# Two hybrid layers on one core: TensorE's order planned in the source by lanes, dilated heads ahead of the latent ones, full-row dilated scores, latent exponentials kept in PSUM

## The chip, the cores and the metric

The kernel runs on one core of one Trainium2 chip. The metric is the device time of one execution in microseconds (us); lower is better. The engines are called as the profile calls them: PE is TensorE (PEld its weight loads), DVE is VectorE, ACT is ScalarE, POOL is GpSimd, SP is SyncE, which issues the DMAs.

## What is computed

Two layers run one after the other over 1024 tokens of width 1024, all in float32. The first adds a pooling mixer and a sliding-window attention; the second adds a latent attention (8 heads, every key) and a dilated attention (24 heads in three groups with dilations 1, 4 and 16, merged by their log-sums). Cut to what matters here:

```python
def hybrid_layer(x, positions, ...):                      # the second layer
    h = rmsnorm_2(x, attn_norm_g)
    proj = h @ w_in
    (c_q, c_kv, k_rope, z_mla, q_dil, k_dil, v_dil, z_dil, g_mla, g_dil) = jnp.split(proj, ...)
    a_out = mla_attention(c_q, c_kv, k_rope, positions, ...)
    y_mla = (a_out * jax.nn.silu(z_mla)) @ w_o_mla
    d_out = dilated_mixture(q_dil, k_dil, v_dil, positions)
    y_dil = (d_out * jax.nn.silu(z_dil)) @ w_o_dil
    merged = sigmoid(g_mla + ...) * y_mla + sigmoid(g_dil + ...) * y_dil
    return x + merged @ w_out

def one_block(q_blk):                                     # latent attention, 128 queries
    s = jnp.einsum('bqhd,bkhd->bhqk', q_blk, k).astype(jnp.float32)
    p = jax.nn.softmax(s, axis=-1).astype(v.dtype)
    return jnp.einsum('bhqk,bkhd->bqhd', p, v)
```

The latent part and the dilated part both need only `h`; the outputs of both meet in `merged`.

## The kernel before

Each float32 operand of a product is split in a high part (a cast to the type `fp32r`) and a low part (the difference), and a product is the sum of high x high, high x low and low x high: three matmuls (`mm3`, lines 136 to 142). ACT makes the high part, DVE the low one (`sub_lo`, lines 115 and 116). A projection of 128 output columns over one half of the tokens is `proj_half` (line 147): 8 x 3 matmuls of 512 columns into one bank of PSUM; its weights come by `load_w` (line 130).

The stages, with the time in the profiled execution at which they stand: norm and transposes of the input (to 25 us), sliding-window attention and pooling (to 292), output projection and second norm (to 402), the small latent projections (to 541), the latent heads (to 986), the dilated heads (to 1600), the two gated output projections (to 1701) and the last projection with the final norm.

*Latent heads* (line 866 on). For each of 8 heads and each half of the queries, 8 key blocks: three score matmuls of 512 columns (891 to 893), exp from PSUM to an SBUF tile `E` (898), a cast to `ph` (901) and a subtraction to `pl` (902, helper line 116), and two block products later in the source the products with the values `vm` (885, 886). POOL adds the `E` tiles for the softmax denominator (907, 925), which `key_sums` (837) finishes with two matmuls of a column of ones. The next head's row maxima come from `row_max` (819), one 512-column matmul and one DVE reduction each; `max_rows` (826) transposes them, negates them and writes them by DMA into row 96 of q, so that the first scores of a head wait for that DMA. `fill()` (line 668) puts other projections (gates, z, v of the dilated heads) between.

*Dilated heads* (line 1093 on). Twelve units, each two heads of one dilation. A unit's q, k and v are projected, q and k turned by `roped` (line 953: a swap by DMA, a product on DVE, one on POOL, a sum on DVE). The q tile of a head holds the high part in the head's 64 rows and the low part in the other 64. k's high part is copied to both halves (`khd`), its low part `kl` is not. So a pair of score matmuls is one of 128 rows and one of 64:

```python
nc.tensor.matmul(o, U.qs[i][:, q], U.kh[i][:, k], start=True, stop=False)
nc.tensor.matmul(o, U.qs[i][r, q], U.kl[r, k], start=False, stop=True)
```

`Head.scores` and `Head.values` (lines 214 and 245) run the two attentions with narrow windows: a masked copy with its maximum on DVE, exp on ACT, transposes of P on PE (291), cast and subtraction (293, 294), products (267). `merge` (1040) joins the three groups of a head through DRAM into `d_d`, which the last stages read.

The order of PE's instructions is not the source's alone. The program is recorded under a scheduler that orders each engine's instructions by its own cost model; the source gives the order in which work is offered (the lists `MLA_FILL`, `MAXES`, `fillers`), and the pools of PSUM banks (`share_banks`, line 90) set how far work can run ahead.

Of the kernel before, what the change touches and what calls it, by code (L numbers as in the profile page):

```python
# [20 lines left out]
C_ID = 0  # L21
C_D1 = 128
C_W = 384
C_M2 = 768
C_IC = 896
C_FREQ = 960
# [41 lines left out]
def hybrid_kernel(  # L68
# [17 lines left out]
    sm = pool("sm", 4)  # L86
    banks = ctx.enter_context(ExitStack())
    pp = psS = psO = psT = None

    def share_banks(p, s, o, t=2):  # L90

        nonlocal pp, psS, psO, psT
        banks.close()
        pp = banks.enter_context(tc.tile_pool(name="pp", bufs=p, space=PSUM))
        psS = banks.enter_context(tc.tile_pool(name="psS", bufs=s, space=PSUM))
        psO = banks.enter_context(tc.tile_pool(name="psO", bufs=o, space=PSUM))
        psT = banks.enter_context(tc.tile_pool(name="psT", bufs=t, space=PSUM))
# [4 lines left out]
    xp = first.enter_context(tc.tile_pool(name="xp", bufs=1))  # L102
    x0 = [xp.tile([128, D], F32, name=f"x{t}") for t in range(8)]
    cc = cst.tile([128, C_N], F32, name="cc")
# [12 lines left out]

    background = []
# [50 lines left out]
    def norm_T(xt, gain, H, t):  # L169

        ss = sm.tile([128, 1], F32, tag="ss", name="ss")
        xn = P_p.tile([128, 1024], F32, tag="P", name="xn")
        nc.scalar.activation(out=xn, in_=xt, func=AF.Square, accum_out=ss)
        rs = rstd_of(ss, D)
        nc.vector.scalar_tensor_tensor(out=xn, in0=xt, scalar=rs, in1=gain, op0=ALU.mult, op1=ALU.mult)
        tok = slice(128 * t, 128 * t + 128)
        for a in range(2):
            ps = psT.tile([128, 4, 128], F32, tag="t", name="pst")
            for j in range(4):
                k = 4 * a + j  # L180
                nc.tensor.transpose(ps[:, j, :], xn[:, 128 * k:128 * k + 128], ident)
            hi = H[0][:, 4 * a:4 * a + 4, tok]
            nc.scalar.copy(hi, ps)
            sub_lo(nc.vector, H[1][:, 4 * a:4 * a + 4, tok], ps, hi)

# [6 lines left out]
    def V_natural(vt, v):  # L192

        for a in range(2):
            ps = psT.tile([128, 4, 2, 64], F32, tag="t", name="pst")
            for j in range(4):
                t = 4 * a + j
                nc.tensor.transpose(flat(ps[:, j]), vt[:, 128 * t:128 * t + 128], ident)
            hi = v[:, 4 * a:4 * a + 4, :, 0]
            nc.scalar.copy(hi, ps)  # L200
            sub_lo(nc.vector, v[:, 4 * a:4 * a + 4, :, 1], ps, hi)


    class Head:
# [6 lines left out]
        def __init__(self, scores_mm, v, tiles, keys, scale, mask, m, den, init=None, fill=()):  # L211
            self.__dict__.update(locals())

        def scores(self):
            self.nm = sm.tile([128, 8], F32, tag="nm", name="nm")
            self.P = []
            for half in range(2):
                P = P_p.tile([128, 4, 256], F32, tag="P", name="P")
                self.P.append(P)
                for (i, a, n) in self.fill:  # L220
                    if i // 4 == half:
                        nc.gpsimd.memset(P[:, i % 4, a:a + n], 0.0)
                for j in range(2):
                    ps = psS.tile([128, 2, 256], F32, tag="s", name="pss")
                    for u in range(2):
                        i = 4 * half + 2 * j + u
                        k0, kw, p0 = self.tiles[i]
                        self.scores_mm(ps[:, u, p0:p0 + kw], slice(128 * i, 128 * i + 128), slice(k0, k0 + kw))
                    for u in range(2):
                        i = 4 * half + 2 * j + u  # L230
                        k0, kw, p0 = self.tiles[i]
                        nc.vector.tensor_tensor_reduce(  # L232
                            out=P[:, 2 * j + u, p0:p0 + kw], in0=ps[:, u, p0:p0 + kw], in1=self.mask(i),
                            scale=1.0, scalar=-3e38 if self.init is None else self.init,
                            op0=ALU.add, op1=ALU.max, accum_out=self.m[:, i:i + 1])
                h4 = slice(4 * half, 4 * half + 4)
                nc.vector.tensor_scalar(out=self.nm[:, h4], in0=self.m[:, h4], scalar1=-self.scale, scalar2=None, op0=ALU.mult)  # L237
                for j in range(4):
                    i = 4 * half + j
                    k0, kw, p0 = self.tiles[i]  # L240
                    a = P[:, j, p0:p0 + kw]
                    nc.scalar.activation(out=a, in_=a, func=AF.Exp, bias=self.nm[:, i:i + 1], scale=self.scale,  # L242
                                         accum_out=self.den[:, i:i + 1])

        def values(self, dest):

            o = [None, None]
            last = {}
            for c, qs in enumerate(self.keys):
                for (i, _) in qs:  # L250
                    last[i // 4] = (c, i)
            opened = set()

            def accumulate(c, h, l, cols):
                runs = []
                for n, (i, _) in enumerate(self.keys[c]):
# [44 lines left out]
            for item in late:  # L301
                accumulate(*item)
# [975 lines left out]
```

## Time and profile before

| what | value |
|---|---|
| median of 3 runs | 1797.91 us (1795.03 to 1797.92) |
| the profiled execution | 1797.49 us |
| its span, first to last instruction | 1795.6 us |
| PE busy | 1712.9 us, 95%, 7900 records |
| PEld busy | 1380.6 us, 77% |
| DVE busy | 1107.9 us, 62% |
| ACT busy | 798.7 us, 44% |
| POOL busy | 430.0 us, 24% |
| DMA | 206.85 MB, mean 115 GB/s |

Busy time is the union of an engine's records. Records of PE overlap, because matmuls are pipelined: the length of one is longer than the step from its start to the next one's start. A time of the profiled execution is read against its own 1797.49 us.

### The profile page before, as it was taken

Reading aid. Unit: us, or ns where it says so; the run is one execution under the profiler, and the core shown is the slowest. Engines: PE = TensorE matmul, PEld = TensorE weight load, DVE = VectorE, ACT = ScalarE, POOL = GpSimd, SP = SyncE. Lnnn points to the kernel's source line nnn. Section 1 sums busy time; section 2 is a strip of 40 time slices with the busy share of each in tenths; the row PEclk is TensorE's granted clock in tenths of the full one; section 3 lists DMA queues with packets and bytes.
Section 4 is the critical chain, followed back from the end, with each engine's and each line's share of the span. In section 5 each row is a group of like instructions: output and inputs, shape, how many; then the busy total and the mean of one; then the engine's idle time right before and its main releaser. Section 6 shows DMA issues by size and latency. Waiting matters only on the chain. (4 is left out here: it accounts for less than half of the span.)

```text
span 1795.6 us, 22168 instructions
## 1 busy us (share of the span) xinstructions
PE 1712.9 (95%) x7900; PEld 1380.6 (77%) x7900; DVE 1107.9 (62%) x1840; ACT 798.7 (44%) x1622; POOL 430.0 (24%) x280
## 2 busy tenths in 40 slices
PE   7999998999999998998989999999999989999998
PEld 6788886888787885776867778777778767877786
DVE  5677764562645677767786576775775567345532
ACT  4455433342332454555555465555555445432121
POOL 1000010011332345546554220230230122032200
PEclk8999998999999998999999999999999989999999
DMA  5311126443344221423132634464463235378642
GB/s 180 80 36 49 49 93 196 136 124 74 88 156 141 68 75 28 113 77 113 50 92 75 166 95 108 119 176 112 114 165 89 76 98 141 126 242 279 188 138 85
DMA packets 189081, 206.85 MB, mean 115 GB/s; under 512 B 29107, under 2 KB 152179, under 8 KB 188844
## 3 DMA queue, kind: packets, MB, share of 16 engines
q1 hardware_dynamic: 188972, 205.45, 39.6%
q8 instruction: 62, 1.02, 0.2%
q14 instruction: 47, 0.39, 0.1%
HBM read 126.86 MB, written 52.27 MB: 100 GB/s over the span
## 5 line engine op out<-in xcount | busy, mean ns | idle before, releaser
L140 PE MATMUL pp<-Hh,whi 128*128 128x512 f32 x1248 | 498.8, 400 | 8.9 <-ACT rt L956 3.0
L142 PE MATMUL pp<-Hh,wlo 128*128 128x512 f32 x1248 | 495.9, 397 | 0.0
L141 PE MATMUL pp<-Hl,whi 128*128 128x512 f32 x1248 | 494.0, 396 | 0.0
L140 PEld LDWEIGHTS pp<-Hh,whi 128*128 128x128 f32 x1248 | 236.5, 190 | 61.3 <-ACT rt L956 4.3
L142 PEld LDWEIGHTS pp<-Hh,wlo 128*128 128x128 f32 x1248 | 236.3, 189 | 51.3 <-issue 0.5
L141 PEld LDWEIGHTS pp<-Hl,whi 128*128 128x128 f32 x1248 | 236.6, 190 | 47.6 <-DVE Hl L116 0.2
L126 ACT CAST whi<-wraw 128x1024 fp32r<-128x1024 f32 (+3 forms) x110 | 109.8, 999 | 221.5 <-PE pp L141 123.6
L116 DVE TENSOR_TENSOR wlo<-wraw,whi 128x1024 fp32r<-128x1024 f32 (+3 forms) x110 | 144.3, 1312 | 94.8 <-ACT whi L126 88.5
L907 POOL TENSOR_TENSOR E<-E 128x1024 f32<-128x1024 f32 x48 | 123.5, 2572 | 208.3 <-ACT E L898 103.2
L116 DVE TENSOR_TENSOR pl<-E,ph 128x512 fp32r<-128x512 f32 x128 | 150.9, 1206 | 31.6 <-ACT ph L901 16.7
L242 ACT ACTIVATE P<-P,nm 128x256 f32<-128x256 f32 (+2 forms) x256 | 118.7, 466 | 96.2 <-DVE nm L237 96.0
L960 POOL TENSOR_TENSOR rsw<-rsw,sinT 128x1024 f32<-128x1024 f32 x24 | 74.7, 3114 | 227.1 <-DMA rsw<-rt 183.0
L824 DVE TENSOR_REDUCE mx<-pst 128x1 f32<-128x512 f32 x128 | 85.5, 683 | 60.7 <-PE pst L823 60.2
L898 ACT ACTIVATE E<-pss 128x512 f32<-128x512 f32 x128 | 74.0, 598 | 71.2 <-PE pss L893 49.6
L116 DVE TENSOR_TENSOR pl<-pst,ph 128x512 fp32r<-128x512 f32 (+2 forms) x120 | 75.5, 639 | 36.1 <-ACT ph L293 35.6
L166 POOL TENSOR_TENSOR rs<-ms,mhalf 128x1 f32<-128x1 f32 (+1 forms) x40 | 23.1, 578 | 278.0 <-DVE ms L164 278.0
L901 ACT CAST ph<-E 128x512 fp32r<-128x512 f32 x128 | 76.6, 622 | 29.3 <-PE pso L885 20.0
L293 ACT CAST ph<-pst 128x512 fp32r<-128x512 f32 (+2 forms) x120 | 64.1, 549 | 54.4 <-PE pst L291 51.3
L232 DVE CUSTOM_DVE_ANT_0 P<-pss,cc 128x256 f32<-128x256 f32 (+2 forms) x192 | 62.6, 369 | 28.1 <-PE pss L1023 22.8
L267 PE MATMUL pso<-ph,v 128*128 128x256 f32 (+1 forms) x280 | 75.3, 287 | 2.5 <-ACT ph L293 2.3
L267 PE MATMUL pso<-pl,v 128*128 128x256 f32 (+1 forms) x280 | 69.4, 285 | 6.2 <-DVE pl L116 6.2
L1022 PE MATMUL pss<-khd,qs 128*128 128x256 f32 (+2 forms) x192 | 64.8, 337 | 6.3 <-DVE qs L116 6.0
(264 smaller groups left out, 3187.1 us busy)
## 6 DMA issues: line engine op xcount, KB each, us to landing
wraw<-in_w_in_dram SPq DMA_DIRECT2D x78, 512.0 KB
rsw<-rt SPq DMA_DIRECT2D x96, 128.0 KB
khd<-kh SPq DMA_DIRECT2D x48, 256.0 KB
wraw<-in_w_out_dram SPq DMA_DIRECT2D x16, 512.0 KB
g_d<-g SPq DMA_DIRECT2D x16, 512.0 KB
og_d<-og SPq DMA_DIRECT2D x12, 512.0 KB
ol<-og_d SPq DMA_DIRECT2D x12, 512.0 KB
bc<-b_d SPq DMA_DIRECT2D x24, 256.0 KB
```

The lines of the kernel that those rows point to most:

```text
L116: eng.tensor_tensor(out=lo, in0=src, in1=hi.bitcast(F32), op=ALU.subtract)
L126: nc.scalar.copy(wh, raw)
L140: nc.tensor.matmul(ps, lh, rh, start=(i == 0), stop=False)
L141: nc.tensor.matmul(ps, lh, rl, start=False, stop=False)
L142: nc.tensor.matmul(ps, ll, rh, start=False, stop=(i == n - 1))
L242: nc.scalar.activation(out=a, in_=a, func=AF.Exp, bias=self.nm[:, i:i + 1], scale=self.scale, accum_out=self.den[:, i:i + 1])
L267: nc.tensor.matmul(o[b][:, q0:q0 + 128 * w], self.v(c), part[:, cols + 128 * n:cols + 128 * (n + w)], start=b not in opened, stop=(part is ...
L824: nc.vector.tensor_reduce(out=mx[:, n, i:i + 1], in_=ps, axis=mybir.AxisListType.X, op=ALU.max)
L898: nc.scalar.activation(out=e, in_=ps, func=AF.Exp, scale=MSC)
L901: nc.scalar.copy(ph, e)
L907: nc.gpsimd.tensor_tensor(out=Es[0], in0=Es[0], in1=E, op=ALU.add)
L960: nc.gpsimd.tensor_tensor(out=sw, in0=sw, in1=sinT, op=ALU.mult)
```

## The change

The arithmetic is the same but for the order of some sums. Four things are different.

1. PE's order is taken from the source (`manual_schedule` for that engine). The source plans it: the stages are generators, "lanes", that yield what they wait for; a `Flow` keeps a clock of constants (.23 us per 512 columns, so much per ACT, DVE and POOL operation) and steps the lane of the lowest number whose needs are met, else the projections in `stream`, else it moves its clock. In the latent stage `pace` limits how many projections may go.
2. The dilated heads stand right behind the second norm, the latent projections and heads behind them. The v projections no longer pass through DRAM.
3. k's low part is copied to both halves as well, and the second score matmul takes all 128 rows.
4. The latent exp is written over its scores in PSUM; cast and subtraction read it there. The product of the high part runs on a bank of its own, that of the low part on another with only the high part of v and a column of ones, whose row is a part of the denominator; POOL adds the high parts alone.

```diff
+    ctx.enter_context(tc.manual_schedule(engines={mybir.EngineType.PE}))
...
+    class Flow:
+        HOP, SLACK = 0.15, 0.7
...
+        def mm(self, n, cols=512):
+            self.now += n * max(0.11, 0.23 * cols / 512)
...
+        def run(self, *until):
+
+            while any(l[2] is not None for l in until):
+                best = None
+                for lane in self.lanes:
+                    ts = [e.t for e in lane[2]]
+                    if None in ts:
+                        continue
+                    at = max(ts, default=0.0)
+                    at += self.SLACK if at > 0.0 else 0.0
+                    if at <= self.now:
+                        best = (self.now, lane)
+                        break
+                    if best is None or at < best[0]:
+                        best = (at, lane)
...
+                at, lane = best
+                if at > self.now:
+                    self.idle.append((self.now, at))
+                    self.now = at
+                self.step(lane)
...
-                nc.tensor.matmul(o, U.qs[i][:, q], U.kh[i][:, k], start=True, stop=False)
-                nc.tensor.matmul(o, U.qs[i][r, q], U.kl[r, k], start=False, stop=True)
+                nc.tensor.matmul(o, self.qs[i][:, q], self.kh[i][:, k], start=True, stop=False)
+                nc.tensor.matmul(o, self.qs[i][:, q], self.kl[i][:, k], start=False, stop=True)
...
+                            for (part, dup) in ((hi, self.kh[i]), (lo, self.kl[i])):
+                                for z in range(2):
+                                    nc.sync.dma_start(dup[64 * z:64 * z + 64].bitcast(F32), part[64 * i:64 * i + 64].bitcast(F32))
...
+    lanes = [F.add(score_lane(heads2), 8), F.add(turn_lane(heads2), 6), F.add(value_lane(heads2), 5)]
...
+    share_banks(4, 2, 0)
+    set_rings(4, 1, 0)
...
-                nc.scalar.activation(out=e, in_=ps, func=AF.Exp, scale=MSC)
-                nc.scalar.copy(ph, e)
-                sub_lo(nc.vector, pl, e, ph)
-                if kb % 2 and kb > 1:
-                    nc.gpsimd.tensor_tensor(out=Es[0], in0=Es[0], in1=E, op=ALU.add)
+                    pace[0] += 14 * MLA_TILES / 128
+                    nc.scalar.activation(out=ps, in_=ps, func=AF.Exp, scale=MSC)
+                    nc.scalar.copy(ph, ps)
+                    sub_lo(nc.vector, pl, ps, ph)
+                    elif kb > 1:
+                        nc.gpsimd.tensor_tensor(out=acc, in0=acc, in1=ph.bitcast(F32), op=ALU.add)
...
-                nc.tensor.matmul(o, v, ph, start=(kb == 0), stop=False)
-                nc.tensor.matmul(o, v, pl, start=False, stop=(kb == 7))
+                    nc.tensor.matmul(o, vm[:, kb, h, 0:128], ph, start=(kb == 0), stop=(kb == 7))
+                    nc.tensor.matmul(o2[0:65], vm[:, kb, h, 64:129], pl, start=(kb == 0), stop=(kb == 7))
...
+    pace[0] = 14 * MLA_FIRST
+    load_qk(0)
+    lanes = [F.add(product_lane(), 5), F.add(exp_lane(), 8), F.add(max_lane(), 7)]
```

Three places of PE's queue show what moved. A row is a source line, the operation, result and operands by the program's names, and the result's size. The first is in the dilated stage, at scores of a unit with 256-column tiles (`khd` and `kl` or `kld` are k's high and low part, `pp` a projection). Before:

```order
L291 MATMUL pst<-idt,P 128x128
L1022 MATMUL pss<-khd,qs 128x256
L1023 MATMUL pss<-kl,qs 128x256
L1022 MATMUL pss<-khd,qs 128x256
L1023 MATMUL pss<-kl,qs 128x256
L1022 MATMUL pss<-khd,qs 128x256
L1023 MATMUL pss<-kl,qs 128x256
L141 MATMUL pp<-Hl,whi 128x512
```

Now:

```order
L463 MATMUL pst<-idt,P 128x128 x8
L1133 MATMUL pss<-khd,qs 128x256
L1134 MATMUL pss<-kld,qs 128x256
L1133 MATMUL pss<-khd,qs 128x256
L1134 MATMUL pss<-kld,qs 128x256
L1133 MATMUL pss<-khd,qs 128x256
L1134 MATMUL pss<-kld,qs 128x256
L1133 MATMUL pss<-khd,qs 128x256
L1134 MATMUL pss<-kld,qs 128x256
L360 MATMUL pp<-Hh,whi 128x512
```

The pairs still alternate; the second of each now takes the tile `kld` with all its rows.

The second place is inside a latent head (`pss` scores, `pst` the next head's row maxima, `pso` products, `pl` the low part of the exponentials). Before:

```order
L891 MATMUL pss<-qh,kh 128x512
L892 MATMUL pss<-ql,kh 128x512
L893 MATMUL pss<-qh,kl 128x512
L844 MATMUL psd<-el,ones 1x512
L885 MATMUL pso<-ph,vm 128x512
L891 MATMUL pss<-qh,kh 128x512
L892 MATMUL pss<-ql,kh 128x512
L893 MATMUL pss<-qh,kl 128x512
L886 MATMUL pso<-pl,vm 128x512
L885 MATMUL pso<-ph,vm 128x512
```

Now:

```order
L1531 MATMUL pst<-kh,qh 128x512
L1647 MATMUL pso<-E,vm 128x512
L1648 MATMUL pso_11309<-pl,vm 65x512
L1611 MATMUL pss<-qh,kh 128x512
L1612 MATMUL pss<-ql,kh 128x512
L1613 MATMUL pss<-qh,kl 128x512
L360 MATMUL pp<-Hh,whi 128x512
L361 MATMUL pp<-Hl,whi 128x512
L362 MATMUL pp<-Hh,wlo 128x512
L1647 MATMUL pso<-E,vm 128x512
L1648 MATMUL pso_11309<-pl,vm 65x512
```

A block's two products now stand together, into two banks, and triples of a projection stand between them and the scores.

The third place is a switch of heads (`mx` are the row maxima that are transposed there). Before, at the switch to the third head:

```order
L844 MATMUL psd<-el,ones 1x512
L830 MATMUL pst<-idt,mx 8x128
L823 MATMUL pst<-kh,qh 128x512 x3
L891 MATMUL pss<-qh,kh 128x512 x3
L823 MATMUL pst<-kh,qh 128x512
```

Now, at the switch to the second head, and so at every other one:

```order
L362 MATMUL pp<-Hh,wlo 128x512
L1539 MATMUL pst<-idt,mx 8x128
L1647 MATMUL pso<-E,vm 128x512
L1648 MATMUL pso_10779<-pl,vm 65x512
L1647 MATMUL pso<-E,vm 128x512
L1648 MATMUL pso_10779<-pl,vm 65x512
L1611 MATMUL pss<-qh,kh 128x512
```

Four products stand between the transpose and the scores that wait for its result. Before, one switch was as close as this; now four are.

## Rows read from the trace of the kernel before

**Rows 1.** The cores: span and mean granted TensorE clock.

```profile
core 0: 1795.6 us, clock 0.979
```

**Rows 2.** Stretches: us, busy us (count) of PE, PEld, DVE, ACT, POOL, clock, DMA.

```profile
0.00:25.00 25.00, 14.23 (x87) 12.65 (x88) 13.73 (x21) 14.44 (x24) 3.60 (x11) 0.87 0.86 273
25.00:292.00 267.00, 256.96 (x1323) 217.61 (x1321) 187.43 (x442) 126.44 (x281) 15.34 (x27) 0.98 0.26 76
292.00:541.00 249.00, 244.97 (x1123) 205.10 (x1124) 121.69 (x181) 80.29 (x173) 47.06 (x60) 0.98 0.40 118
541.00:986.00 445.00, 421.06 (x1749) 326.42 (x1747) 310.54 (x334) 221.88 (x384) 207.06 (x89) 0.98 0.29 84
986.00:1600.00 614.00, 594.91 (x2855) 473.19 (x2856) 388.54 (x753) 315.58 (x700) 125.39 (x68) 0.98 0.47 126
1600.00:1701.00 101.00, 93.28 (x382) 73.52 (x382) 52.51 (x57) 22.66 (x25) 25.82 (x18) 0.97 0.77 246
1701.00:1796.00 95.00, 87.45 (x386) 72.07 (x384) 33.45 (x55) 17.39 (x38) 5.70 (x9) 0.99 0.34 111
```

**Rows 3.** Line 140: min/median/max ns, first and last start us.

```profile
L140 PE MATMUL y<-Hh,whi x128: 389/389/393, 1701.2 to 1787.6; 128*128 128x512 f32 x128
```

**Rows 4.** Timeline of PE, latent heads: start us, length us, instruction.

```profile
709.24 0.39 PE L891 MATMUL pss<-qh,kh 97*128 97x512 f32 x1
709.47 0.40 PE L892 MATMUL pss<-ql,kh 97*128 97x512 f32 x1
```

**Rows 5.** Timeline, first attention, two starts one pair apart.

```profile
76.00 0.28 PE L502 MATMUL pss<-ks,qs 128*128 128x256 f32 x1
...
76.24 0.28 PE L502 MATMUL pss<-ks,qs 128*128 128x256 f32 x1
```

**Rows 6.** Timeline of PE and PEld, dilated scores.

```profile
1150.19 0.28 PE L1022 MATMUL pss<-khd,qs 128*128 128x256 f32 x1
1150.40 0.18 PEld L1023 LDWEIGHTS pss<-kl,qs 64*128 64x128 f32 x1 [0.25 <-issue]
1150.40 0.38 PE L1023 MATMUL pss<-kl,qs 64*128 64x256 f32 x1
...
1150.71 0.39 PE L1022 MATMUL pss<-khd,qs 128*128 128x256 f32 x1
...
1151.03 0.38 PE L1023 MATMUL pss<-kl,qs 64*128 64x256 f32 x1
```

**Rows 7.** Line 1023: min/median/max ns of its weight loads.

```profile
L1023 PEld LDWEIGHTS pss<-kl,qs x192: 182/183/285, 1009.0 to 1542.0; 64*128 64x128 f32 x192
```

**Rows 8.** DVE groups by shape: busy us, mean ns, idle before.

```profile
L116 DVE TENSOR_TENSOR pl<-E,ph 128x512 fp32r<-128x512 f32 x128 | 150.9, 1206 | 31.6 <-ACT ph L901 16.7 <-PE pso L886 11.4 <-PE pso L885 2.1
...
L116 DVE TENSOR_TENSOR pl<-pst,ph 128x512 fp32r<-128x512 f32 x96 | 64.6, 684 | 34.8 <-ACT ph L293 34.5
```

**Rows 9.** Timeline of POOL, then of DVE, latent heads.

```profile
706.36 8.29 POOL L907 TENSOR_TENSOR E<-E 128x1024 f32<-128x1024 f32 x3 [16.30 <-DVE pl L116]
...
710.14 5.06 DVE L116 TENSOR_TENSOR pl<-E,ph 128x512 fp32r<-128x512 f32 x2
```

**Rows 10.** Waits from 597 to 986 us: total, times, longest.

```profile
PEld pso L886 <- DVE pl L116: 18.3, 19, 2.2
...
PE pso L886 <- DVE pl L116: 10.6, 9, 1.8
```

**Rows 11.** ACT groups by shape: busy us, mean ns, idle before.

```profile
L898 ACT ACTIVATE E<-pss 128x512 f32<-128x512 f32 x128 | 74.0, 598 | 71.2 <-PE pss L893 49.6 <-DVE el L116 7.6 <-POOL E L907 5.7
L293 ACT CAST ph<-pst 128x512 fp32r<-128x512 f32 x96 | 54.7, 585 | 47.9 <-PE pst L291 45.3 <-PE pso L267 1.9
```

**Rows 12.** Timeline at a head switch of the latent stage.

```profile
694.41 0.41 PE L830 MATMUL pst<-idt,mx 128*8 128x128 f32 x1
...
697.10 0.27 ACT L832 ACTIVATE mt<-pst 8x128 fp32r<-8x128 f32 x1 [1.27 <-DMA den_d<-den]
...
699.23 0.80 PE L891 MATMUL pss<-qh,kh 97*128 97x512 f32 x1 [0.69 <-DMA qh<-mt]
```

More of the change, by code (lines that the diff above doesn't have):

```diff
@@ L167, in rstd_of @@
         return rs
[L169 to L184, printed above, removed]
     def new_H():
@@ new lines, in hybrid_kernel, with stream_lane @@
+    F.between = ahead
+    def stream_lane():
+        while True:
+            yield (stream,)
+            it = stream.pop(0)
+            current[:] = [it]
+            for i, (n, rhs, evac, need) in enumerate(it.parts):
+                yield (R.pp, Of(lambda: it.ready[n].t if n < len(it.ready) else None)) + tuple(need)
+                slot = R.pp.take()
+                ps = pp.tile([128, 512], F32, tag="pp", name="pp")
+                yield from paced(ps, [((it.w[n][0][:, k], it.w[n][1][:, k]), r) for k, r in enumerate(rhs) if r])
+                slot.t = evac(ps)
+                for m in {p[0] for p in it.parts[:i + 1]} - {p[0] for p in it.parts[i + 1:]}:
+                    if it.slots[m].t is None:
+                        it.slots[m].t = F.now
+            for s in it.slots:
+                if s.t is None:
+                    s.t = F.now
@@ new lines, in hybrid_kernel, with wake @@
+    nc.sync.dma_start(cc, consts[:, :C_ID])
+    scl = cst.tile([128, 4], F32, name="scl")
+    nc.sync.dma_start(scl, pool_scale[0].rearrange("(g p) -> p g", p=128), allow_slow_non_contiguous=True)
+    nc.vector.tensor_scalar(out=scl, in0=scl, scalar1=0.5, scalar2=None, op0=ALU.mult)
+    def wake(n):
+        ps = psO.tile([128, 4, 128], F32, tag="o", name="wake")
+        for j in range(n):
+            nc.tensor.matmul(ps[:, j % 4], ident, ident, start=True, stop=True)
+    wake(12)
+    F.now = 9.0
@@ L682, in hybrid_kernel @@
+    F.run(*lanes)
+    F.run(*[l for l in F.lanes if l[0] == 11])
+    sc.close()
+    qtab, ktab, krT, gc = (P_p.tile([128, 1024], F32, tag="P", name=n) for n in ("qtab", "ktab", "krT", "gc"))
     nc.gpsimd.memset(qtab[0:64], 1.0)
@@ L911, in hybrid_kernel @@
-                    if kb == SUMS and sums is not None:
-                        sums()
-                    if (half, kb) in MLA_FILL[h]:
-                        fill()
-                    if (half, kb) == (1, 3) and h and h % 2 == 0:
-                        finish(h // 2 - 1)
-                for item in late:
-                    product(*item)
+                    F.mm(3)
+                    pace[0] += 14 * MLA_TILES / 128
+                    ph = E[:, kb % 2]
+                    pl = pt_p.tile([128, 512], F32R, tag="ph" if kb % 4 == 3 else "pl", name="pl")
```

1961 lines of the change are left out of this document (1182 added, 779 removed).

## The prediction

> **What bounds the kernel now.** The cores view comes first: one core, a span of 1795.6 us, a mean granted TensorE clock of .979 [rows 1]. The profiled execution took 1797.5 us, 1.9 us outside its span, and lies .4 us under the median of the three runs (1797.9), so a time below is a span plus 1.9. A measurement of this kernel can tell some .2% (3.6 us) from no change.
>
> Next the busy time by stretch [rows 2]: TensorE (PE) is busy 87 to 98% of every stretch after the start, VectorE (DVE) and ScalarE (ACT) never over 71%. That busy time hides part of what can be won, because a matrix instruction's record lasts longer than the step to the next. So I count steps. In the last stretch the first and last `y<-Hh` of line 140 start at 1701.2 and 1787.6 with 381 steps between them: .227 us for 512 columns [rows 3]. Among latent scores it is .23 [rows 4]. A pair of two 256-column score matmuls in the first attention takes .24, so .12 each [rows 5].
>
> The built program has 7872 matmuls: 5864 of 512 columns, 192 of 416, 656 of 256, 32 of 192 and 1128 of 128. At .23, .19 (.23 x 416/512), .12, .10 (192 columns) and .10 (128 columns; between .06, half of .12, and .12) they come to 1349 + 36 + 79 + 3 + 113 = 1580 us if every one ran at its step and none waited. The span is 216 us longer. Where those are:
> - 12 us at the ends: no matmul starts in the first 4.7 us, and the last one starts 7.5 us before the end.
> - some 63 us in the dilated scores, next paragraph.
> - some 141 us of waits and of the lower clock. From 541 to 986 us (latent heads) 1749 instructions, nearly all of 512 columns, need 402 us of 445: 43 lost. From 986 to 1600 (dilated heads) the program's 1645 long, 448 of 256, 32 of 192 and 730 short ones need 508 of 614: 106 lost, 63 of them the scores', so 43. From 1600 to 1701, 382 long ones need 88 of 101: 13. That leaves 42 before 541 us, 11 of them in the first 25 us.
>
> **Full-row scores.** In a dilated pair line 1022 multiplies 128 rows, line 1023 a 64-row half of q with a 64-row k low part. Where the 64-row one follows, its weight load stands marked "issue", waiting for nothing the profile shows, and starts only with its matmul; then the steps are .31, .32 [rows 6] against .12 for the same width in full rows [rows 5]. The difference, .19, is the length of a weight load (.18 at least, [rows 7]). The change copies k's low part to both halves (line 1214, tiles `kld`), so both matmuls of a pair have 128 rows. There are 192 pairs, 384 instructions. Upper bound: all lose .19, 73 us. Lower bound: the first of each pair loses only the .09 seen where it follows other work (1150.19 to 1150.40, [rows 6]) and the second .19: 54. I take 63, the middle, as both forms are frequent. It lands in full only if PE bounds the stretch, and DVE's 389 us and ACT's 316 of 614 leave that room [rows 2]. The price is four more 256 KB copies for each of 12 units. DMA engines are busy .47 of that stretch, and 16 passes of v through DRAM (8 stores, 8 loads) fall away, so I cost them at nothing; were the copies late, the k lane, 14.8 us and more of planned work ahead of its scores, would be late next.
>
> **Latent exponentials in PSUM.** Before, exp writes E to SBUF, ACT casts it, and DVE subtracts two SBUF operands: 1.21 us in the mean, against .68 for the same width with one operand in PSUM [rows 8]. Two such subtractions take 5.06 us while GpSimd (POOL) adds E tiles [rows 9]. PE pays: its low products and their weight loads wait 10.6 + 18.3 us for that DVE line, the two overlapping [rows 10]. The change keeps E in its bank, so the subtraction has one PSUM operand: 128 x .52 = 67 us less DVE, and PE's wait, some 15 us of the 43, goes. ACT's exp (.60) and cast (.59 by the nearest row) stay [rows 11]. New: a product group has two banks and two more evacuations a half head, and POOL adds 112 half-width tiles (1.4 us each, half of 8.29/3, [rows 9]) where it added 48 full and 16 half ones. Each of the sixteen halves has some 17 us of PE work in the new order; exp and casts take 8 x 1.19 = 9.5 of ACT there, subtractions and maxima 8 x 2 x .68 = 11 of DVE, the adds 10 of POOL, and the projections' evacuations come on top: covered, not by much.
>
> **Order and lanes.** Positions are from the built order, PE work counted in the steps above. In the dilated stage the nearest value product stood .4 us of PE work behind its transposes; now at least 2.4, against a cast of .59 and a subtraction of .68 [rows 8, 11]. So most of the 43 us there should go; I leave 17 for rope and copies, which the plan prices by constants. In the latent stage some get worse: the low product follows its score's end by 3.0 to 14.3 us before and 1.5 to 6.2 now, while exp, cast and subtraction need .60 + .59 + .68 and their handovers, some 2.3. The sixteen last products of a half stand at 1.5 to 2.8, up to .8 short; I take .5 each: 8. And at four of seven head switches only 1.0 us of work lies between the transposed row maxima and the scores that need them. Before, the one switch like that (.75) held PE from 694.4 to 699.2, of which 2.1 from ACT's negation to the first score [rows 12]. Four at 2.1 + .2 - 1.0 are 5 us (lower bound), at 3.8 each 15; I take 8. So of 43: 15 go, 16 come back by name, the other 28 shrink to 10 because the gate and z projections are paced through the stage. That is 26.
>
> Dilated first, latent second: the merge of the three groups moves off the end. In the old tail PE lost 13 us, with `d_d` late; now the latent outputs are the late ones, but over 50 us of gate and dilated-output matmuls stand between the last key sums and the first matmul that reads those outputs. I leave 5. Start (11) unchanged: same loads. 25 to 541 us: 31 become 24, with attention, pooling and the two output loops in the same sequence.
>
> **Sum.** 1580 + 12 + (11 + 24 + 26 + 17 + 5 = 83) = 1675 of span, **1677 us**: 63 from scores, 58 from waits.
>
> **Rivals.**
> - *The order buys nothing, only the pairs do.* Waits stay at 141: 1797.5 - 63 = **1735**. For it: a fixed PE queue stops for one late lane wherever the plan's constants are wrong, and POOL stretches DVE work that the plan prices evenly. Against: PE's waits on DVE `pl` are removed at their source. .16
> - *The full rows give nothing.* A narrower row group would then cost no more than a full one, and the .31 steps would come from something else in the stage: 1677 + 63 = **1740**. The rows say otherwise: same widths, types and neighbours, and .12 against .31. .04
>   The Trainium skill, page "TensorE: Matmul & The Clock Gate", section "Part 3: Packing small matmuls — row/col tiling", says that a weight load overlaps running matmuls only where its row group differs. By that rule the old 64-row load would be the one that hides and this edit a loss of cover; this trace disagrees (rows 5 and 6).
> - *Nearly all waits go*, 141 to under 40: about **1630**. For it: the projections of gates and z can fill almost any gap. Against: start, switches and last products named above. .12
> - *Slower: the latent score tile holds its bank too long.* Scores, maxima and key sums share four banks, and a score bank is now held through exp, cast and subtraction, 2.3 us, where it was free after exp. With the maximum's 1.2 that is 3.5 of 8.2 bank-us in each of 128 key blocks (2.06 us of PE work each). It decides when a bank is held over 7 us: a subtraction queued behind two SBUF pairs that POOL stretches (2.5 each, [rows 9]) reaches that. To end over 1798 each block must lose .95 us, a hold of 10.8. .06, with other plan failures of that size in it.
>
> **How the numbers follow.** Forecast .62 (1640 to 1715), the two at 1735 to 1740 .20, 1630 .12, slower .06. The range must hold 8 in 10: the upper end, 1740, takes in the lower bound for scores or most of the waits; the lower, 1630, the upper bound (73) with 37 fewer us of waits. Left out: half of the .12, a third of the .20, the .06. Faster by over .2%: .92; within .2%: .02, a coincidence of both failures; slower: .06.
>
> **What would show it.** Right: in the dilated stage both score lines step by .12 at 256 columns and no weight load there waits on "issue"; the latent subtraction stays at .68 with no spread; PE does not wait for `pl`; the stage of latent heads loses under 30 us against its count, with gaps at every second head switch. Wrong: PE's busy share in either heads' stage under 93%, DVE or ACT over 85% in the latent stage, scores waiting for banks, or a weight load of line 1134 still exposed.

## The result and the profile after

The changed kernel takes **1854.3 us** (median of 4 runs, 1845.7 to 1854.8) against 1796.5 (1793.7 to 1797.9): a ratio of 1.031, 95% interval 1.028 to 1.034, **slower**. The forecast was 1677 us, faster. The profiled execution is the quickest of the four, 1845.7 us with a span of 1843.6.

The stretches of the changed kernel, as in [rows 2] (us; PE, PEld, DVE, ACT, POOL busy; mean granted clock; DMA share; GB/s). They are the attention and pooling, the output loop, the dilated stage, the latent projections, the latent stage and the gated outputs:

```profile
28.00:297.00 269.00, 256.79 (x1313) 217.12 (x1313) 185.83 (x452) 123.79 (x281) 17.36 (x19) 0.98 0.23 70
297.00:409.00 112.00, 110.01 (x491) 89.06 (x492) 60.32 (x86) 39.86 (x78) 9.04 (x19) 0.97 0.47 146
409.00:1141.00 732.00, 632.12 (x3220) 537.58 (x3219) 389.80 (x761) 325.15 (x717) 117.73 (x62) 0.93 0.45 113
1141.00:1272.00 131.00, 123.62 (x569) 105.25 (x568) 66.79 (x101) 40.73 (x96) 49.23 (x51) 0.97 0.50 142
1272.00:1612.00 340.00, 321.19 (x1301) 239.15 (x1300) 225.95 (x333) 210.11 (x368) 198.81 (x133) 0.96 0.28 83
1612.00:1750.00 138.00, 129.20 (x542) 102.38 (x541) 57.48 (x68) 35.51 (x43) 27.73 (x18) 0.96 0.65 210
```

PE is busy 86% of the dilated stage, DVE 53%, ACT 44%. To see what each stage loses, I take every step from one matmul's start to the next in the trace, less the plain step of its width (.23, .19, .121, .10, .097 us for 512, 416, 256, 192 and 128 columns). What is left is the excess; of a step taken at the lower granted clock, up to one more plain step is put down to the clock. The forecast's terms beside it, in us of excess and clock together; the last column is experiment e14, told of below:

| stretch | forecast | after | e14 |
|---|---|---|---|
| start | 11 | 15.2 | 15.1 |
| 25 us on to the dilated stage, and the latent projections | 24 | 38.8 | 44.0 |
| dilated stage | 17 | **143.6** (114.3 + 29.3 of the clock) | 65.2 |
| latent stage | 26 | 42.2 | 46.2 |
| from there to the end | 5 | 12.5 | 13.0 |
| sum | 83 | 252 | 183 |

The sum of the plain steps is 1579 us, one less than forecast. So the count was right and the waits were wrong. Of the prediction's signs against itself one shows, PE under 93% in a heads' stage. Of its signs for itself two are missing: the latent stage loses 42 us and not under 30, and the latent low products still wait for `pl`, 6.1 us where it was 10.6 [rows 10].

The two edits inside the stages did what they were to do. The timeline of PE in the dilated stage, at the upper level of the clock (2.4 GHz), and at a place where the granted clock is .50 (1.2 GHz); behind it the stretches around that place (PE busy, granted clock, DMA share, GB/s):

```profile
699.40 0.28 PE L1133 MATMUL pss<-khd,qs 128*128 128x256 f32 x1
699.52 0.28 PE L1134 MATMUL pss<-kld,qs 128*128 128x256 f32 x1
699.63 0.28 PE L1133 MATMUL pss<-khd,qs 128*128 128x256 f32 x1
```

```profile
520.70 0.42 PE L1133 MATMUL pss<-khd,qs 128*128 128x256 f32 x1
520.91 0.41 PE L1134 MATMUL pss<-kld,qs 128*128 128x256 f32 x1
```

```profile
508.90:514.70 5.80, 0.35 (x2) 0.87 0.00 1
514.70:519.00 4.30, 3.33 (x15) 0.50 0.00 0
519.00:523.00 4.00, 4.00 (x19) 0.50 0.52 135
523.00:530.00 7.00, 7.00 (x36) 0.97 0.00 0
```

Full rows step by .12 instead of .31 and .32 [rows 6], and by .21 where the clock is low, which it is after PE stood for 5.8 us. The latent subtraction, 1.21 us in [rows 8], is in the page's groups at

```profile
L119 DVE TENSOR_TENSOR pl<-pss,E 128x512 fp32r<-128x512 f32 x128 | 86.0, 684 | 63.0 <-ACT E L1619 62.7
```

PE's large waits are now in the dilated stage (waits from 409 to 1141 us: total, times, longest; first of PE, then the four longest of SP's queue):

```profile
PE pss L1133 <- DVE qs L119: 58.6, 9, 8.3
...
PE pp L360 <- ACT rt L1167: 32.4, 7, 16.3
```

```profile
SPq L134 <- DVE wlo L119: 167.0, 14, 16.2
SPq L1154 <- DVE og L1150: 77.3, 10, 14.6
SPq L1214 <- ACT rt L1167: 64.6, 9, 9.7
SPq L1172 <- ACT rt L1167: 46.3, 5, 16.5
```

Scores wait for q (line 1133), and projections (line 360) wait for ACT to clear their bank (`rt`, line 1167). SP's longest waits need not be the harmful ones: those of line 134 (weight loads) and line 1154 stay, at 162.5 and 77.9 us, in e14, which is 79 us faster. Two places show how PE's waits come about. The chain of the changed kernel from 736 us (start, length, what; pieces under .1 us left out) has k's copies (line 1214), then the rope swap of q (line 1172), and then everything that stands on it, 15 us until the first score:

```profile
736.10 1.21 SPq L1214
737.41 1.17 SPq L1172
738.63 0.98 SPq L1172
739.67 0.58 SPq L1172
740.29 2.54 DMA rsw<-rt
742.99 3.40 POOL rsw L1174
746.41 1.24 DVE rt L1175
747.73 1.92 ACT qs L1191
749.67 1.87 DVE qs L119
751.59 0.47 PE pss L1133
```

The longest stop of PE, 16.5 us behind the matmul at 1013.5, has another form. SP's timeline, then ACT's:

```profile
1011.12 2.01 SPq L1214 DMA_DIRECT2D khd<-kh  x3
...
1016.22 1.78 SPq L1214 DMA_DIRECT2D kld<-kl  x2
1018.10 1.21 SPq L1304 DMA_DIRECT2D ol<-og_d  x1
1019.40 1.66 SPq L1306 DMA_DIRECT2D bc<-b_d  x2
```

```profile
1029.56 1.07 ACT L1167 COPY rt<-pp 128x512 f32<-128x512 f32 x2 [12.39 <-POOL ol L1307]
```

`rt` has nothing to do with `ol`, a tile of the merge. But both are taken from the pool `cp` (the helper `C()`), whose six slots (buffers of 4 KB in each partition) go round: in the changed kernel a unit takes seven turns (rt, rsw, kh and now kl for k, rt and rsw for q, vt for v), and each third unit ten more for the merge (cx, ct, cw, three times ol and bc, zl). ACT's copy waits until POOL has multiplied `ol` with `bc`, whose load was issued behind the eight k copies. Meanwhile the projection's bank is full and PE's next instruction is another projection.

### The profile page after: what moved, and what is told of

Its sections match the earlier page's. It is cut to its first block, busy times and chain, and to the rows that moved or that the text cites. A ratio compares the mean times of both kernels' runs of the same rounds, so it can differ in the third digit from the quotient of the medians.

```text
span 1843.6 us, 22364 instructions
## 1 busy us (share of the span) xinstructions
PE 1674.4 (91%) x7892; PEld 1375.2 (75%) x7892; DVE 1036.8 (56%) x1884; ACT 809.4 (44%) x1647; POOL 435.3 (24%) x328
## 4 chain that ended last, share of the span: by engine, by line
PE 48%; DVE 6%; DMA 6%; issue 5%; SPq 4%; ACT 4%; POOL 2%; POOLq 0%; DVEq 0%; ACTq 0%
PE pp L360 9%; PE pp L361 8%; PE pp L362 8%; PE pso L493 2%; DMA bc<-b_d 2%; SPq L1214 2%; DMA rsw<-rt 2%; PE y L362 2%; PE y L360 2%; PE y L361 2%; PE pss L1612 2%; PE pss L1611 1%; POOL rsw L1174 1%; PE pss L1613 1%; SPq L1172 1%
## 5 line engine op out<-in xcount | busy, mean ns | idle before, releaser
L360 PE MATMUL pp<-Hh,whi 128*128 128x512 f32 x1248 | 511.6, 410 | 40.5 <-ACT rt L1167 32.4
L360 PEld LDWEIGHTS pp<-Hh,whi 128*128 128x128 f32 x1248 | 242.4, 194 | 90.7 <-ACT rt L1167 35.0
L127 ACT CAST whi<-wraw 128x1024 fp32r<-128x1024 f32 (+1 forms) x108 | 109.2, 1011 | 249.8 <-PE pp L361 144.7
L119 DVE TENSOR_TENSOR wlo<-wraw,whi 128x1024 fp32r<-128x1024 f32 (+1 forms) x108 | 135.5, 1255 | 124.1 <-ACT whi L127 114.6
L1174 POOL TENSOR_TENSOR rsw<-rsw,sinT 128x1024 f32<-128x1024 f32 x24 | 77.9, 3244 | 395.1 <-DMA rsw<-rt 364.3
L1629 POOL TENSOR_TENSOR acc<-acc,E 128x512 f32<-128x512 f32 x96 | 129.9, 1353 | 64.2 <-ACT E L1619 61.2
L119 DVE TENSOR_TENSOR pl<-pss,E 128x512 fp32r<-128x512 f32 x128 | 86.0, 684 | 63.0 <-ACT E L1619 62.7
L1133 PE MATMUL pss<-khd,qs 128*128 128x256 f32 (+2 forms) x192 | 55.6, 310 | 58.6 <-DVE qs L119 58.6
L1618 ACT ACTIVATE pss<-pss 128x512 f32<-128x512 f32 x128 | 73.9, 584 | 74.7 <-PE pss L1613 64.2
L1173 DVE TENSOR_TENSOR rt<-rt,cosT 128x1024 f32<-128x1024 f32 x24 | 34.3, 1431 | 110.7 <-DMA rsw<-rt 110.7
L1133 PEld LDWEIGHTS pss<-khd,qs 128*128 128x128 f32 x192 | 41.7, 217 | 64.8 <-DVE qs L119 62.5
```

The source lines that it names most:

```text
L119: eng.tensor_tensor(out=lo, in0=src, in1=hi.bitcast(F32), op=ALU.subtract)
L127: nc.scalar.copy(wh, raw)
L360: nc.tensor.matmul(ps, lh, rh, start=(i == 0), stop=False)
L1133: nc.tensor.matmul(o, self.qs[i][:, q], self.kh[i][:, k], start=True, stop=False)
L1174: nc.gpsimd.tensor_tensor(out=sw, in0=sw, in1=sinT, op=ALU.mult)
L1618: nc.scalar.activation(out=ps, in_=ps, func=AF.Exp, scale=MSC)
```

## Experiments

Lines are those of the changed kernel unless said. "Excess" is counted as above, clock apart. Every time is a median, every ratio one to the kernel before in runs of the same group, with its interval. The medians of the kernel before lie between 1794.2 and 1799.4 us in the five groups, so a difference of some 6 us between times of two groups is not resolved.

**e1 to e4: which part of the change loses?** Four edits of the changed kernel.

```diff
-   nc.sync.dma_start(sw[32 * b:32 * b + 32], t[...])          # e1
+   nc.scalar.dma_start(sw[32 * b:32 * b + 32], t[...])
-   nc.sync.dma_start(dup[64 * z:64 * z + 64]..., part[...])   # e2
+   nc.gpsimd.dma_start(dup[64 * z:64 * z + 64]..., part[...])
-   nc.tensor.matmul(o, self.qs[i][:, q], self.kl[i][:, k], start=False, stop=True)   # e3
+   nc.tensor.matmul(o, self.qs[i][r, q], self.kl[r, k], start=False, stop=True)
-   ctx.enter_context(tc.manual_schedule(engines={mybir.EngineType.PE}))   # e4
```

e1. 

> Edit: the four transfers of each rope swap (rsw<-rt) are issued by ScalarE, which writes rt just before, and no longer by SyncE; all else as in the changed kernel (1854). Theory Q (SyncE's queue runs in order, and the swaps stand in it behind weight loads, og stores and k copies that wait): POOL's wait for rsw falls from 364 us to under 180 (before: 183), the excess steps into the first score matmul of the dilated stage (60 us) fall under 25, and the time to 1770 to 1805, although ScalarE pays 96 issues of some .6 us. Rival P (TensorE's written order is too tight, whatever feeds it): scores stay late, 1835 to 1860. Rival C (the added copies load the DMA engines): the copies are all still there, 1840 to 1860.

e2. 

> Edit: the eight copies of a unit (khd, kld) are issued by GpSimd, no longer by SyncE; all else as in the changed kernel (1854). Theory Q: SyncE loses 96 issues of .5 to 1.3 us and 85 us of waits in front of them, but weight loads and og stores (167 + 77 us of waits) still stand ahead of the swaps: 1800 to 1835. Rival P: 1840 to 1860. Rival C: bytes and transfers are the same, 1845 to 1860.

e3. 

> Edit: full-row scores undone alone (64-row low product, one kl tile, four copies a unit fewer); all else as in the changed kernel (1854). The pairs would again take .31 + .31 instead of .13 + .13 where nothing stands in front. Rival C (the copies cost more than the pairs gave): under 1830, towards 1797. Theory Q: the queue loses 48 issues, some 45 us of SyncE's time, of which perhaps half was in front of TensorE, and the pairs take back 54 to 73: 1870 to 1905. If the score stalls are only slack behind some other late thing: about 1854.

e4. 

> Edit: TensorE's instructions are ordered by the scheduler, as the other engines' are, instead of standing in the planned order; all else as in the changed kernel (1854). Rival P (the planned order is what stalls): under 1810. Theory Q: the same tiles are late; the scheduler can put other work in front where it sees them late, but it sees them by its own durations: 1830 to 1880, with POOL's wait for rsw still over 250 us.

Measured: e1 **1871.7** (1.041, 1.035 to 1.047); e2 **1836.9** (1.023, 1.018 to 1.028); e3 **1858.3** (1.034, 1.030 to 1.039); e4 **1837.8** (1.024, 1.020 to 1.028).

e1 misses its forecast on the wrong side. The score waits did fall, the excess into line 1133 from 60 to 18 us, but ACT now waited with the swaps in its own queue, and line 360 waits longer for it:

```profile
PE pp L360 <- ACT rt L1167: 48.1, 10, 21.7
...
PE pss L1133 <- DVE qs L119: 14.4, 5, 6.1
```

e2 keeps bytes and slots and wins 17 us, 2 us short of theory Q's range. e3 is the surprise: without the full rows the pairs step by .31 again, and the time moves by 4 us, as in the third of its cases. Either the score stalls are slack behind something else, or the four added copies and the slot of `kl` take back about what the pairs give; e5 and e10 try both, in the old order. e4 wins 17, within theory Q's range: the fixed order has its price, and it is not the main one.

**e5 and e6: each part alone, in the old order.**

```diff
+   lo = C("kl", F32R)                        # e5, kernel before
+   U.kl = [dq.tile([128, S], F32R, tag="kl", name="kld") for i in range(2)]
...
+   for (part, dup) in ((hi, U.kh[i]), (lo, U.kl[i])):
...
-   nc.scalar.activation(out=e, in_=ps, func=AF.Exp, scale=MSC)      # e6, kernel before
+   nc.scalar.activation(out=ps, in_=ps, func=AF.Exp, scale=MSC)
```

e5. 

> Edit: the kernel before with full-row scores alone (k's low part copied to both halves, eight copies a unit, kl through one of the six slots that rt, rsw, kh and vt share); its order, its latent exponentials and everything else stay. The identity's 128 columns leave the constants tile, for room. Theory P2 (the loss of the change lies in its new order, where q is projected just before its scores): the prediction's 1735 holds, 1730 to 1755. Rival C2 (the copies and the slot take back what the pairs give, in any order): 1780 to 1815.

e6. 

> Edit: the kernel before with the latent exponentials in PSUM alone: exp in place, the cast to ph in the tile of the pair, GpSimd adds ph tiles half by half; the order and the dilated stage stay. The key sums lack the low part of E, so the output is not the reference's. The prediction's terms: VectorE's subtraction from 1.21 to .68 us, TensorE's 15 us of waits on it go: 1775 to 1790. Rival: banks held longer with three score banks instead of sooner freed ones: 1797 to 1830.

Measured: e5 **1825.5** (1.017, 1.014 to 1.020), e6 **1789.3** (.997, .995 to .999). Beside the lines shown, e5 and the later edits of the kernel before leave the identity's 128 columns out of the constants tile, as the changed kernel does; e6 does not. In e6, e11, e13 and e15 the key sums leave out the low part of the exponentials. The prediction's 1735 for the full rows alone was off by 90 us, and on the other side of the old time: theory P2 falls. The loss is there without the new order, even above rival C2's range. The chain of e5 from 1119 us, at a stop before scores (its lines: 986 the copies, 958 the swap), reads like the one above:

```profile
1119.01 1.14 SPq L986
...
1122.05 1.16 SPq L986
...
1123.31 0.55 SPq L958
...
1125.84 4.08 DMA rsw<-rt
...
1130.14 3.37 POOL rsw L960
```

But in this order PE loses most at the value products, 60 of the stage's 102 us of excess. The longest stop there shows another way from a late swap to PE. The cosine product of the rope (line 959) is written over the tile that the swap reads, so it waits for the swap; `pl` of the value products stands behind it on DVE (DVE's timeline, then PE's):

```profile
1220.95 1.22 DVE L959 TENSOR_TENSOR rt<-rt,cosT 128x1024 f32<-128x1024 f32 x1 [9.63 <-DMA rsw<-rt]
...
1225.38 0.68 DVE L116 TENSOR_TENSOR pl<-pst,ph 128x512 fp32r<-128x512 f32 x1
```

```profile
1226.11 0.58 PE L267 MATMUL pso<-pl,v 128*128 128x256 f32 x1 [7.61 <-DVE pl L116]
```

The chain to it again has k's copies, from 1205.0 us, and loads of the merge ahead of the swap. These waits of DVE are 30.5 us in the dilated stage before and 57.7 in e5, 110.7 in the changed kernel and 34.4 in e14.

The exponentials alone (e6) bring 5 us, inside their range, of the 15 that PE's wait was worth.

**e7 and e8: more margin in the plan.** Only the plan's constants change.

```diff
-   box[1] = F.chain(("g", 3.1), ("v", 1.3), at=e + 2.5)
+   box[1] = F.chain(("g", 3.1), ("v", 1.3), at=e + 6.5)     # e8: 10.5
-   self.kev.t = F.chain(("a", 1.7), ("v", 1.8), at=box[1]) + 3.0
+   self.kev.t = F.chain(("a", 1.7), ("v", 1.8), at=box[1]) + 8.0     # e8: 12.0
```

e7. 

> Edit: in the plan of the changed kernel the rope swap's constant goes from 2.5 to 6.5 us and the k copies' from 3.0 to 8.0; nothing else is changed, so TensorE's order is replanned with q's scores later against q's projection. Theory P2 (the plan puts each unit's first scores exactly where it believes q to be there, without margin, and believes too early by some 4 to 10 us): excess steps into the first score matmul fall from 60 us to under 30, time 1800 to 1835. Theory Q (SyncE's queue holds the swap for 10 to 20 us at a time): 1840 to 1865, since no constant covers that.

e8. 

> Edit: as the one before, with 10.5 and 12.0 us. Theory P2: the score stalls go nearly all (under 15 us), but the plan itself now idles where nothing else is allowed to go on: 1790 to 1840. Theory Q: the waits move with the work, 1830 to 1865.

Measured: **1858.1** and **1867.2** (1.035, 1.031 to 1.038; 1.041, 1.037 to 1.044). e7 lies in theory Q's range, e8 2 us above it. In e7 the score stalls went as foreseen, from 60 to 7 us, and the stage's excess rose from 114 to 119 us: PE waited at value products and v's transposes instead.

```profile
PE pso L493 <- DVE pl L119: 31.2, 10, 6.1
...
PE pst L518 <- ACT vt L1235: 24.2, 3, 10.8
```

So where the scores stand in PE's order is not what sets the stage's length.

**e9 to e12: the copies' queue, and full rows without them.** e9 is e5 with the copies on POOL. e10 writes k's low part into one half of a tile whose other half was zeroed once, so that the low product has 128 rows with no copy of it; e11 adds e6's exponentials; e12 is e10's edit in the changed kernel.

```diff
-   nc.sync.dma_start(dup[64 * z:64 * z + 64]..., part[...])     # e9
+   nc.gpsimd.dma_start(dup[64 * z:64 * z + 64]..., part[...])
+   kz = [[dt1.tile([128, S], F32R, ...) for n in range(1 + i)] for i in range(2)]   # e10
+   nc.gpsimd.memset(tl[64 - 64 * i:128 - 64 * i].bitcast(F32), 0.0)
...
+   U.kl = [kz[0][0], kz[1][(3 * U.j + U.g) % 2]]
+   sub_lo(nc.vector, grouped(U.kl[i][r], U.g), perm(a[r], U.g), grouped(hi[r], U.g))
```

e9. 

> Edit: the kernel before with full-row scores, as in the run that took 1825.5, but its eight copies a unit are issued by GpSimd instead of SyncE. Theory S (the copies cost by standing in SyncE's queue ahead of q's rope swap, .5 to 1.3 us each): most of the loss goes, 1750 to 1790. Rival B (their bytes, or kl's shared slot): same bytes, same slot, 1810 to 1830.

e10. 

> Edit: the kernel before with full-row scores and no copy of the low part: VectorE writes k's low part of each head into its own half of a 128-row tile whose other half was set to zero once, so the low product has 128 rows, four copies a unit as before. Two VectorE subtractions of 64 rows take the place of one. Theory S with the prediction's price of the pairs: 1797 - 63, 1725 to 1750. Rival L (the pairs' steps only cover other waits of the stage, which come out once they are short): 1775 to 1800.

e11. 

> Edit: as e10, and the latent exponentials in PSUM as in e6 (key sums without the low part of E). If the two are independent: e10's time less 4 to 8 us. A larger gain would say that the stages are coupled through the filling projections.

e12. 

> Edit: the changed kernel with the zeroed halves of e10 in place of the four kld copies a unit; TensorE's planned order is unchanged. Theory S: full rows stay and the queue is as short as in the run with half rows (1858), so 1858 - 54 to 73: 1785 to 1810, still no faster than the kernel before, because q's chain is late in this order anyway. Rival O (this order loses whatever the copies do): 1835 to 1860.

Measured: e9 **1790.1** (.996, .994 to .998), e10 **1781.1** (.990, .987 to .993), e11 **1766.5** (.983, .981 to .984), e12 **1839.2** (1.023, 1.020 to 1.026).

e9 against e5: the same bytes and slots, another issuer, 35 us, to the upper edge of theory S's range. Rival B falls for this order. The Trainium skill, page "DMA: Bandwidth & Descriptors", section "Issuing engines are not separate DMA queues", says that a second issuing engine saves only the sequencer's time to initiate a DMA, usually small beside the DMA itself. An issue is indeed shorter than its DMA here (in e9 .52 us against 5.4 to landing, in the median). Yet SP is busy for 82 us with the 96 issues in e5 (`kld` 1.03 us each in the median), and q's swap stands behind them. That SP's queue also waits for slots is seen in e9, where a swap waits for the landing of copies that it does not read:

```profile
SPq L958 <- DMA khd<-kh: 25.0, 10, 5.9
```

e10 is rival L's result: of 63 us for the pairs 15 arrive, although they step by .12; the excess into the value products rises from 18 us before to 36. e11 wins 15 more where 4 to 8 were expected, so the two edits help each other. e12 lies in rival O's range, but it has a fault of my own: its single tile for the first head is written late three times,

```profile
PE pss L1138 <- DVE kz L119: 44.6, 3, 15.2
```

so it cannot be laid to the order; e14 does without that tile.

**e13 to e15: order and k path, two by two.** e13 is the kernel before with e5's and e6's edits. What is left between it and the changed kernel is the order and the lanes, but also the second bank of the latent products, the low part of the key sums, the shares of the PSUM banks and v's way through DRAM; "new order" below stands for all of these. The "lean" k path of e14 (changed kernel) and e15 (kernel before, with e6's edit):

```diff
-   hi, lo = C("kh", F32R), C("kl", F32R)
+   nc.gpsimd.memset(self.kl[i][64 - 64 * i:128 - 64 * i].bitcast(F32), 0.0)
...
+   nc.scalar.copy(grouped(self.kh[i][r], self.g), perm(a[r], self.g))
+   sub_lo(nc.vector, grouped(self.kl[i][r], self.g), perm(a[r], self.g), grouped(self.kh[i][r], self.g))
...
+   nc.sync.dma_start(self.kh[i][z].bitcast(F32), self.kh[i][r].bitcast(F32))
```

e13. 

> Edit: the kernel before with both other parts of the change, full-row scores by eight copies a unit and the latent exponentials in PSUM (key sums without the low part of E), in its own order. It differs from the changed kernel in the order and the lanes alone. Additive theory: 1825.5 less the 5 of the exponentials alone, 1815 to 1825, so that the new order and its lanes cost 30 to 40 us of the changed kernel's 1854. Rival (the loss is all of the copies', the order is neutral): 1845 to 1860. Rival (copies hurt only this order): under 1810.

e14. 

> Edit: the changed kernel, its planned order untouched, with k's high part written by ScalarE straight into the two kh tiles (two ops of 64 rows) and the low part by VectorE into two of three rotating tiles whose other half GpSimd sets to zero: two copies a unit instead of eight, and neither kh nor kl in the six shared slots. Theory S+ (the queue and the shared slots are what makes k, q and the projections' evacuations late): the dilated stage's excess falls from 114 us to under 70, 1785 to 1810. Rival O (the order itself loses): 1825 to 1845, near the 1839 of the zeroed halves.

e15. 

> Edit: the kernel before, in its own order, with the lean k path of e14 and the exponentials in PSUM (key sums without the low part of E): full rows, two copies a unit where before had four. Theory S+: under the 1766 of e11, 1745 to 1762, since queue and slots were in front of TensorE before too. Rival (before had slack there; only its own step times are left): 1762 to 1772.

| full rows, exponentials in PSUM | eight copies | lean |
|---|---|---|
| old order | e13 **1810.9** (1.009, 1.006 to 1.011) | e15 **1756.4** (.978, .975 to .981) |
| new order | **1854.3** (1.031, 1.028 to 1.034) | e14 **1775.7** (.989, .985 to .993) |

e13 lies 4 us under the additive range, e14 9 us under its own, e15 inside theory S+'s. The k path costs 55 us in the old order and 79 in the new; the new order costs 43 us with the copies and 19 without. With the lean path the changed kernel is 1.1% faster than the kernel before. Its dilated stage (same columns as above):

```profile
409.00:1066.00 657.00, 618.14 (x3237) 524.22 (x3236) 423.36 (x775) 347.37 (x731) 136.80 (x84) 0.98 0.37 98
```

Up to the same point of the program the stage is 75 us shorter, PE is busy 94% instead of 86, and the clock is back at .98.

**e16 to e18: queue or slots, order or place, and the version to keep.** e16 writes both parts of k straight into their tiles, as e14, and fills the other halves by eight transfers a unit.

```diff
+   for dup in (self.kh[i], self.kl[i]):                       # e16
+       for c in (slice(0, 512), slice(512, 1024)):
+           nc.sync.dma_start(dup[z, c].bitcast(F32), dup[r, c].bitcast(F32))
-   ctx.enter_context(tc.manual_schedule(engines={mybir.EngineType.PE}))   # e17: e14 with this
```

e16. 

> Edit: the changed kernel, planned order untouched, with k's high and low parts written straight into the kh and kl tiles (no shared slot for either), and the other halves filled by four transfers, each split in two column halves: eight issues a unit on SyncE as in the changed kernel, half their bytes, no slot. Theory Queue alone: the eight issues stand in front of the swaps as before, 1830 to 1850. Theory Slots alone: 1770 to 1790, as with the lean path (1775.7). Both needed together: 1800 to 1825.

e17. 

> Edit: e14 (the changed kernel with the lean k path) with TensorE's instructions ordered by the scheduler instead of the plan. Rival P (the fixed order pays for each late tile): 17 us less as with the copies, 1755 to 1765. If the plan is sound once k and q come in time: 1775 or more.

e18. 

> Edit: the kernel before with the lean k path alone; the whole computation, exponentials as before. By the earlier gains of the exponentials (5 us alone, 15 with full rows): 1760 to 1772, so faster than the kernel before by 1.3 to 2%.

Measured: e16 **1781.8** (.990, .987 to .993), e17 **1775.6** (.986, .982 to .989), e18 **1760.9** (.979, .974 to .983).

All three lie in ranges named beforehand: slots alone, a sound plan, and the 1760 to 1772 of e18. e16 parts queue and slots as far as these runs do: eight issues a unit on SP without the slots cost at most some 6 us over the lean path, the slots with the issues on POOL (e2) 61. The two waits of PE in the dilated stage, 58.6 and 32.4 us in the changed kernel, are in e16:

```profile
PE pss L1133 <- DVE qs L119: 11.1, 5, 3.4
...
PE pp L360 <- ACT rt L1167: 3.9, 1, 3.9
```

e16 moves half the bytes of the changed kernel's copies, and its 96 issues hold SP for 54 us where those of the changed kernel take 84. So a share of the bytes and of the issue time in its gain is not excluded; bytes alone were not tried. Why the issuer was worth 35 us in the old order (e9) and 17 in the new (e2) is open. e17 equals e14, as far as the 6 us between groups allow: once tiles come in time, no price of the fixed order shows, and the 19 us between the orders are not its fixing. Where they are was not tried by itself. The traces of e14 and e15 put 46 us of excess and clock against 28 on the latent stage, 44 against 28 on the first attention, the output loop and the latent projections, 65 against 85 on the dilated stage. e18, the whole computation in the old order, beats both kernels by some 36 and 93 us.

## Why the prediction was wrong

- **Count and steps**: right. 1579 us of plain steps, .12 in both score lines, no "issue" wait there.
- **The copies, "I cost them at nothing"**: this step failed. It looked at the DMA engines' busy share (.47) and not at what the copies hold: a place in SP's queue, .5 to 1.3 us an issue, and two of six shared slots. In the old order they cost 44 us (e5 against e10), 35 of them gone with the issuer (e9); in the new one the whole k path costs 79 (e14), and 73 of them go in e16, which keeps the eight issues but takes no slot and moves half the bytes. The prediction said that the k lane "would be late next" in this case, but did not price it, and the late things, at the two places followed above, were q's swap and a projection's evacuation, which stand behind the copies.
- **Full rows, -63**: the size was right, for the steps of the pairs in the trace of the kernel before hold 64 us of excess without the waits; the condition "only if PE bounds the stretch" did not hold. 15 us arrive without copies (e10), 36 with the lean path, which also spares two copies and a slot (e18). In e10 part of the rest comes back as waits before the value products, 18 us more.
- **Exponentials in PSUM**: subtraction at .68 as forecast; the gain is 5 us alone (e6), 15 beside e5 or e10 (e13, e11), and too small to tell between the groups beside the lean path (e15, e18), where 15 stood in the sum.
- **Dilated waits 43 to 17**: they became 144, and 65 even on the lean path. Reading distances in PE work assumed that everything else takes only its own time; the waits of queue and slots have no place in that. More margin in the plan moved the stalls without shortening the stage (e7).
- **Latent stage 26**: 42. The two product lines lose 20 us, 18 before, where 15 should have gone and 8 stood for the last products; 8.8 of them are a wait for the cast `E` on ACT, 6.1 for `pl`. The lower clock adds 11; the head switches are small, 3.5 us before the first score line. PE does not wait for score banks there, so the mechanism of the rival that ended slower, the bank held too long, was not what happened.
- **Clock**: the granted clock fell from .98 to .93 in the dilated stage. The lower level costs 55 us in all, against 26 before; no term of its own stood for that.

The rival "nothing but the pairs" (1735) was refuted with the forecast: e5 shows that the pairs as made here lose.

## What to carry to other kernels

A copy that rides on DMA engines with time to spare can still cost, as here, by its place in the issuer's queue and by the buffer that it holds until it lands: list who shares the buffer pool and who stands behind in the queue before costing it at nothing. Where an edit saves engine time but needs a duplicate, look for one that needs none; zeros in the unused half gave the full-row rate here without a copy (.12 a step in e10). When more margin in one place moves a stall to another and leaves the stage's length, look for a shared resource before the order.

## What the runs showed that was not expected

A wait that grows need not cost: POOL waits 183 us for `rsw` in the profiled execution of the kernel before, 315 in e16, which is faster. The same copy takes longer to issue on SP (median 1.07 us for `kld` in the changed kernel) than on POOL (.51 in e2) or than its halves without the slots (.57 in e16). And a late tile can cost twice, for here PE came back at the lower clock: the scores at 520.70 still step by .21, 6 us after such a wait.
